# Output projection by token tile, earlier down-projection operands, and the last block's gate moved into its weights

## The chip, the cores and the metric

One core of a Trainium2 chip runs the whole layer. The metric is device time in microseconds (us). The kernel before takes 1323.11 us, the median of three runs (1322.59, 1323.11, 1325.68). Engines are called as in the profile: PE is TensorE (matmuls), PEld its weight loads, DVE VectorE, ACT ScalarE, POOL GpSimd, SP SyncE (here the engine that issues most DMAs).

## The reference, cut to what matters

One transformer layer over 1024 latent tokens of width 1024, in float32. A retention branch and a latent-attention branch come first (not touched by the change); their outputs `y` are concatenated. Then:

```python
x_mid = x + gt_a * (concatenate([y_ret, y_mla]) @ w_out)         # w_out 1024 x 1024
h     = modulate(rms_norm(x_mid, g_ffn), sh_f, sc_f)
x     = x_mid + gt_f * (square(relu(h @ w_ff1)) @ w_ff2)         # 1024 -> 4096 -> 1024
return rms_norm(x, g_final)
```

`gt_a` and `gt_f` are gates: one number per output column (1024 each), the same for all tokens.

## The kernel before, in words

**Products.** Matmul operands are float32 values split into a rounded high part and a low rest. `split` (L102) does that: ACT casts the value (L103), DVE subtracts the cast from it (L104). One product of two operands is then three matmuls (`mm3`, L98 to L100): high by high, high by low, low by high. Tokens are handled in eight tiles of 128 (t = 0 to 7).

**Slots.** Nearly all larger buffers are 4 KB per partition and come from a list of 45 slots (`sl.get`, `sl.put`). A slot is handed out in the order in which slots are given back in the program's text, so a load waits until whoever held its slot before is through. The program is written as one list of steps; the build then lists the instructions of each engine by program order and a modelled time of readiness, so an instruction can stand somewhat ahead of its place in the text. An engine runs its list in order. SP's queue issues loads and stores in its own order, and a load that waits holds up what stands behind it.

**Output projection (630 to about 690 us).** The weights `w_out` are loaded in eight pieces: two column halves hf of 512 columns, four pieces of 256 rows each. `load_wo` loads a piece, POOL multiplies it by the gate `gt_a` of its columns, and `split_wo` (up to three pieces later) splits it. `load_y` loads and splits a token tile of `y`, and loads the tile of `x` into `acc[t]`. `wout_mm(hf, t)` is one group: 24 matmuls of 128x512 for tile t and column half hf, whose result DVE adds into `acc[t]` (the read-out of PSUM, `tt` at L94). The loop goes over both halves, and in each over the tiles: (0, 2) to (0, 7), then (1, 0) to (1, 7); the groups (0, 0) and (0, 1) are done inside the attention before. After a tile's second half come its sum of squares on ACT, the reciprocal root (`rstd_of`: small DVE and ACT operations), the scaling (L1301), the store of `acc[t]` to DRAM as `xm[t]`, and, one tile later, `h2_post`: eight transposes on PE and eight scalings by `Af` (four on DVE at L1064, four on ACT) that write `h` as `h2r`.

**Up products (about 690 to 990 us).** Each 2x2 block product is done by seven products in place of eight (q = 1 to 7, a Strassen scheme). The operands made of `h` are four quarters B11, B12, B21, B22 and four combinations T1 to T4 (`pairop`, L1081, on DVE or POOL, then `bsplit`). B11 and B21 need tokens 0 to 511 only; T1 = B12 - B11, T2 and T4 need tokens 512 to 1023 too. There are 16 blocks p of `w_ff1` with 7 products of 12 matmuls each, in the order `order`; `post1` reads the results out of PSUM, applies the squared relu on ACT and stores the seven left operands of the down products to DRAM (`ud`: a, y, z, w) through SP's queue.

**Down products (about 990 to 1306.6 us).** Four blocks b of `w_ff2` (1024 rows each), seven products each in the order q = 2, 1, 6, 5, 3, 7, 4: 28 steps of 48 matmuls (`mm_2`, four groups k of 12). `load_u` loads the left operand of a step from `ud`, two steps ahead; `load_w2(b)` loads the eight raw weight pieces of a block; `chain_w2` and `chain2_w2` make T1 to T4 of them on POOL (eight operations of 128x1024); `prep2` splits both operands of a step (four casts, four subtractions of 128x1024), one step ahead. After each group DVE adds the result into the quarters of `acc` to which that product belongs (for b = 0 the first is a copy on ACT).

**End.** In the last block the residual tiles `xm` are loaded into `xr_` (`load_xm`) and the gate `gt_f` into `bc[5]` (`load_bc5`). `gated` multiplies a half tile of `acc` by the gate (on DVE or POOL, L1255), adds the residual, and ACT sums the squares; `final` takes the reciprocal root and scales the tile (L1269) into `xr_`, which is stored as the output. Tiles 0 to 3 go through this after product 3, tiles 4 to 7 after products 7 and 4.

## Time and profile before

| | |
|---|---|
| median of three runs | 1323.11 us |
| the profiled execution | 1324.64 us, of which its span is 1322.8 |
| busy share of the span | PE 96%, PEld 82%, DVE 72%, ACT 49%, POOL 19% |
| mean granted clock of PE | 0.989 of full speed |
| last matmul ends | 1306.6 us |

The busy share counts the time in which an engine executes something. An engine that is busy can still be slowed by what it shares with others, so the mean duration of an operation is to be read beside it. A window is a stretch of the span, in us from its start. In a list of waits, "PE ps L99 <- DVE u L104" is PE at line 99, which stood until an operation of DVE at line 104 was done. In a timeline, a row that ends in xN holds N neighbouring instructions, and its second number is their time together.

### The profile page before, as it was taken

How to read it: one execution, taken by the hardware profiler on the slowest of the kernel's cores; microseconds unless marked ns; L12 is line 12 of the kernel's file. 1: busy time of each engine (PE TensorE's matmuls, PEld its weight loads, DVE VectorE, ACT ScalarE, POOL GpSimd, SP SyncE). 2: the span in 40 equal slices, each digit the busy share in tenths (PEclk: the TensorE clock that was granted, in tenths of full speed). 3: DMA queues.
4: the chain of work that ended last, by engine and by line, in shares of the span. 5: the costliest groups of instructions: out<-in, count | busy, mean ns of one | idle time of the engine just before them, and what ended most of it. 6: DMA issues, size and time to landing. Idle time of an engine off the chain costs nothing.

```text
span 1322.8 us, 18063 instructions
## 1 busy us (share of the span) xinstructions
PE 1274.1 (96%) x6665; PEld 1089.7 (82%) x6665; DVE 950.9 (72%) x1828; ACT 654.8 (49%) x1365; POOL 252.9 (19%) x151
## 2 busy tenths in 40 slices
PE   7999999999999999799989999999998999999995
PEld 7788888999989898688777888888886888888884
DVE  5798576665787777985687755565549687888888
ACT  2851257754455555432466655555546543343442
POOL 0100000000000000311343133233315060603501
PEclk9999999999999999999998999999999999999998
DMA  9508401300001003362421544544485635454443
GB/s 346 217 1 279 167 28 53 101 13 1 1 9 37 9 25 102 130 199 96 144 81 64 189 139 157 160 154 134 154 276 182 225 101 175 149 177 143 141 146 128
DMA packets 77547, 166.40 MB, mean 126 GB/s; under 512 B 7689, under 2 KB 27858, under 8 KB 77458
## 3 DMA queue, kind: packets, MB, share of 16 engines
q1 hardware_dynamic: 74338, 156.56, 35.0%
q0 software_dynamic: 2544, 8.15, 1.8%
q8 instruction: 52, 0.85, 0.3%
q10 hardware_dynamic: 576, 0.53, 0.1%
q14 instruction: 37, 0.30, 0.1%
HBM read 123.53 MB, written 41.69 MB: 125 GB/s over the span
## 4 chain that ended last, share of the span: by engine, by line
PE 83%; DVE 11%; DMA 2%; issue 2%; ACT 1%; POOL 0%; POOLq 0%; SPq 0%; DVEq 0%; ACTq 0%
PE ps L99 23%; PE ps L98 23%; PE ps L100 23%; DVE u L104 3%; DVE u L94 3%; PE ps L895 2%; PE ps L280 2%; PE ps L858 1%; PE ps L862 1%; PE ps L860 1%; PE ps L861 1%; PE ps L859 1%; PE ps L238 1%; DVE u L1269 1%; DMA u<-uda 1%
## 5 line engine op out<-in xcount | busy, mean ns | idle before, releaser
L99 PE MATMUL ps<-u,u 128*128 128x512 f32 (+3 forms) x1664 | 615.4, 370 | 10.0 <-DVE u L104 6.8
L98 PE MATMUL ps<-u,u 128*128 128x512 f32 (+3 forms) x1664 | 619.9, 373 | 4.0 <-DVE u L94 2.3
L100 PE MATMUL ps<-u,u 128*128 128x512 f32 (+3 forms) x1664 | 613.9, 369 | 3.6 <-DVE u L104 1.9
L99 PEld LDWEIGHTS ps<-u,u 128*128 128x128 f32 x1664 | 315.1, 189 | 61.8 <-DVE u L104 9.2
L98 PEld LDWEIGHTS ps<-u,u 128*128 128x128 f32 x1664 | 314.8, 189 | 56.7 <-DVE u L94 3.4
L100 PEld LDWEIGHTS ps<-u,u 128*128 128x128 f32 x1664 | 314.7, 189 | 54.6 <-DVE u L104 2.7
L104 DVE TENSOR_TENSOR u<-u,u 128x1024 fp32r<-128x1024 f32 (+4 forms) x213 | 290.7, 1383 | 66.4 <-ACT u L103 55.8
L94 DVE TENSOR_TENSOR u<-ps,u 128x512 f32<-128x512 f32 (+4 forms) x334 | 210.8, 650 | 122.7 <-ACT u L1153 56.8
L103 ACT CAST u<-u 128x1024 fp32r<-128x1024 f32 (+3 forms) x215 | 197.2, 941 | 190.5 <-PE ps L99 46.4
L1081 POOL TENSOR_TENSOR u<-u,u 128x1024 f32<-128x1024 f32 x34 | 100.9, 2990 | 182.9 <-ACT u L103 98.9
L863 DVE TENSOR_REDUCE mx<-ps 128x1 f32<-128x512 f32 (+1 forms) x96 | 55.4, 595 | 26.7 <-PE ps L862 26.5
L94 DVE TENSOR_TENSOR u<-u,u 128x512 f32<-128x512 f32 x72 | 50.6, 702 | 33.0 <-ACT u L1131 18.4
L897 ACT CAST u<-ps 128x512 fp32r<-128x512 f32 (+1 forms) x96 | 45.3, 530 | 22.9 <-PE ps L895 22.8
L103 ACT CAST u<-tmp 128x512 fp32r<-128x512 f32 x64 | 37.8, 621 | 37.3 <-DVE u L104 31.9
L1095 POOL TENSOR_TENSOR tmp<-u,u 128x512 f32<-128x512 f32 x16 | 20.7, 1296 | 176.2 <-DMA u<-in_w_ff_dram 172.8
L933 POOL DMA_DIRECT2D y_dram<-tmp x7 | 5.4, 765 | 253.5 <-ACT tmp L931 253.5
L874 ACT ACTIVATE u<-ps,nm 128x512 f32<-128x512 f32 x64 | 43.7, 693 | 17.8 <-DVE nm L867 17.8
L104 DVE TENSOR_TENSOR u<-tmp,u 128x512 fp32r<-128x512 f32 x64 | 43.8, 722 | 11.8 <-ACT u L103 9.0
L1130 ACT ACTIVATE u<-u 128x512 f32<-128x512 f32 x64 | 40.1, 628 | 19.0 <-DVE u L94 18.8
L1131 ACT ACTIVATE u<-u 128x512 f32<-128x512 f32 x64 | 40.3, 631 | 1.4
L858 PE MATMUL ps<-u,u 128*128 128x512 f32 (+1 forms) x96 | 37.5, 391 | 2.7 <-ACT u L874 2.5
L427 DVE SCALAR_TENSOR_TENSOR u<-u,sc,u 128x1024 f32<-128x1024 f32 x28 | 35.9, 1281 | 4.2 <-DMA u<-in_w_ada_dram 3.7
(210 smaller groups left out, 1339.4 us busy)
## 6 DMA issues: line engine op xcount, KB each, us to landing
u<-in_w_ff_dram SPq DMA_DIRECT2D x64, 512.0 KB, 4.4
u<-in_w_ada_dram SPq DMA_DIRECT2D x48, 512.0 KB, 5.3
u<-in_x_dram SPq DMA_DIRECT2D x16, 512.0 KB, 5.6
udy<-u SPq DMA_DIRECT2D x16, 512.0 KB, 3.0
udz<-u SPq DMA_DIRECT2D x16, 512.0 KB, 3.4
udw<-u SPq DMA_DIRECT2D x16, 512.0 KB, 3.9
u<-udy SPq DMA_DIRECT2D x16, 512.0 KB, 6.5
u<-udz SPq DMA_DIRECT2D x16, 512.0 KB, 4.6
```

The costliest lines, as they stand in the source:

```text
L94: V.tensor_tensor(out=o, in0=a, in1=b, op=op)
L98: T.matmul(ps, lhsT=lh, rhs=rh, start=start, stop=False, **kw)
L99: T.matmul(ps, lhsT=lh, rhs=rl, start=False, stop=False, **kw)
L100: T.matmul(ps, lhsT=ll, rhs=rh, start=False, stop=stop, **kw)
L103: S.copy(out=hi, in_=raw)
L104: (eng or V).tensor_tensor(out=lo, in0=raw, in1=f(hi), op=ALU.subtract)
L858: T.matmul(ps[:, 0:n], lhsT=qh, rhs=kh, start=True, stop=False)
L863: V.reduce_max(out=mx[:, kb:kb + 1], in_=ps[:, 0:n], axis=AX.X)
L874: S.activation(out=dst[kb], in_=ps[:, 0:n], func=AF.Exp, scale=SCALE, bias=nm, accum_out=su[:, kb:kb + 1])
L897: S.copy(out=hi, in_=ps[:, 0:m, :])
L1081: eng.tensor_tensor(out=o[v][0], in0=a[v][0], in1=b[v][0], op=op)
L1131: S.activation(out=ap, in_=ap, func=AF.Square)
```

## The change

Three edits, in one diff.

1. *Output projection.* The groups keep their contents and get another order, `wseq`: (0, 2), (0, 3), then (1, 0) to (1, 3), then the two halves of tile 4, of tile 5, of tile 6 and of tile 7 next to each other. The four loads of the second column half's weights are issued before the first two of these groups, and the loads of `y`, the first splits of `h` (`bsplit`), the first loads of `w_ff1` and their preparation move to places in the new sequence.
2. *Down operands.* The left operand of the first down step and the first weight quarter are loaded 11 products ahead of the end of the up products instead of 6, the rest 6 and 4 ahead of it. The first step's splits are placed 6 products ahead of that end instead of 3, and the second step's, which stood at the first down step, 2 ahead of it.
3. *Gate.* For the last block, `gate_w2` multiplies the eight raw weight pieces by the gate `gt_f` on POOL, so that the block's products need no gate. What the first three blocks have summed up in `acc` is multiplied by the gate and added to the residual by `to_mid` on DVE: halves of tiles 0 to 3 at the last two steps of the third block, of tiles 4 to 7 at the first two steps of the last. The gate's load, and the loads of the last block's weights in each block (at product 5 in place of product 3), move accordingly. `gated` is gone; `squares` and `final` are left for the end, and the output is scaled in place in `acc`.

```diff
--- before.py
+++ after.py
@@ -1172,8 +1172,8 @@
 
     w2r, w2v = {}, w_ff2.rearrange("(g i p) c -> i p g c", i=2, p=P)
 
-    def load_w2(b):
-        for q in ("B21", "B11", "B12", "B22"):
+    def load_w2(b, qs=("B21", "B11", "B12", "B22")):
+        for q in qs:
             i, j = BH[q]
             w2r[b, q] = [sl.get((2, 512)) for _ in range(GB // 2)]
             for v, r in enumerate(w2r[b, q]):
@@ -1250,15 +1250,6 @@
 
     fs = {}
 
-    def gated(t, cs, eng=None):
-        w, xw = acc[t][0][:, cs], xr_[t][0][:, cs]
-        (eng or V).tensor_tensor(out=w, in0=w, in1=bc[5][0][:, cs], op=ALU.mult)
-        tt(w, w, xw, ALU.add)
-        if t not in fs:
-            fs[t] = sm(2, "ss2")
-        h = cs.start // 512
-        S.activation(out=xw, in_=w, func=AF.Square, accum_out=fs[t][:, h:h + 1])
-
     def final(t):
         ss = fs[t]
         tt(ss[:, 0:1], ss[:, 0:1], ss[:, 1:2], ALU.add)
@@ -1266,59 +1257,59 @@
         n = 2 if t == NT - 1 else 1
         for q in range(n):
             cs = slice(q * 1024 // n, (q + 1) * 1024 // n)
-            V.scalar_tensor_tensor(out=xr_[t][0][:, cs], in0=acc[t][0][:, cs], scalar=r, in1=gfin[0][:, cs],
+            V.scalar_tensor_tensor(out=acc[t][0][:, cs], in0=acc[t][0][:, cs], scalar=r, in1=gfin[0][:, cs],
                                    op0=ALU.mult, op1=ALU.mult)
-            (nc.sync, nc.scalar)[q].dma_start(out=out[0, t * P:(t + 1) * P, cs], in_=xr_[t][0][:, cs])
+            (nc.sync, nc.scalar)[q].dma_start(out=out[0, t * P:(t + 1) * P, cs], in_=acc[t][0][:, cs])
 
     lag = Lag(1)
-    for hf in range(2):
-        for t in range(NT):
-            if hf == 0:
-                for _ in range(2):
-                    mod_step()
-                    mod_load(4, 32)
-                if 4 <= t + 2 < NT:
-                    load_y(t + 2)
-                if t in (3, 4, 5, 6):
-                    load_wo(1, t - 3)
-                if t == 7:
-                    wlag.flush()
-            if hf or t >= 2:
-                wout_mm(hf, t, pG)
-            if hf == 1:
-                sl.put(*yt_[t])
-                if t == 0:
-                    Af = const.tile([P, KD], F32, name="Af")
-                    V.scalar_tensor_tensor(out=Af, in0=mcol[4], scalar=1.0, in1=col("gf"), op0=ALU.add, op1=ALU.mult)
-                if t % 4 == 0:
-                    for u in range(4):
-                        h2r[u, t // 4] = sl.get((2, 512))
-                sq = sl.get((1024,))
-                ss = sm(1, "ss")
-                S.activation(out=sq[0], in_=acc[t][0], func=AF.Square, accum_out=ss)
-                nc.gpsimd.dma_start(out=xm[t], in_=acc[t][0])
-                r = rstd_of(ss, D, 1, "x")
-                V.tensor_scalar(out=sq[0], in0=acc[t][0], scalar1=r, scalar2=None, op0=ALU.mult)
-                sl.put(acc[t])
-                wt = slice((t % 4) * P, (t % 4 + 1) * P)
-                lag.push(lambda t=t, sq=sq, wt=wt: h2_post(t, sq, wt))
-                if t == 2:
-                    mod_fin(fins.popleft())
-                if t == 4:
-                    load_w1(0)
-                    load_w1(1)
-                if t == 5:
-                    bsplit("B21", braw("B21"))
-                    bsplit("B11", braw("B11"))
-                if t == 6:
-                    chain_w1(0)
-                    for q in (2, 1):
-                        for p in range(2):
-                            prep1(p, q) if (p, q) != (1, 1) else None
-        for u in range(4):
-            sl.put(*wo.pop((hf, u)))
-        if hf == 0:
+    wseq = [(0, 2), (0, 3), (1, 0), (1, 1), (1, 2), (1, 3)] + [(hf, t) for t in range(4, NT) for hf in range(2)]
+    for n, (hf, t) in enumerate(wseq):
+        if n < 8:
+            for _ in range(2):
+                mod_step()
+                mod_load(4, 32)
+        if n < 2:
+            load_wo(1, 2 * n)
+            load_wo(1, 2 * n + 1)
+            wlag.flush()
+        if n < 2 or (hf, t) in ((0, 4), (0, 5)):
+            load_y({0: 4, 1: 5}.get(n, t + 2))
+        if n == 2:
             sl.put(bc[2])
+        wout_mm(hf, t, pG)
+        if n == 9:
+            while fins:
+                mod_fin(fins.popleft())
+        if hf == 1:
+            sl.put(*yt_[t])
+            if t == 0:
+                Af = const.tile([P, KD], F32, name="Af")
+                V.scalar_tensor_tensor(out=Af, in0=mcol[4], scalar=1.0, in1=col("gf"), op0=ALU.add, op1=ALU.mult)
+            if t % 4 == 0:
+                for u in range(4):
+                    h2r[u, t // 4] = sl.get((2, 512))
+            sq = sl.get((1024,))
+            ss = sm(1, "ss")
+            S.activation(out=sq[0], in_=acc[t][0], func=AF.Square, accum_out=ss)
+            nc.gpsimd.dma_start(out=xm[t], in_=acc[t][0])
+            r = rstd_of(ss, D, 1, "x")
+            V.tensor_scalar(out=sq[0], in0=acc[t][0], scalar1=r, scalar2=None, op0=ALU.mult)
+            sl.put(acc[t])
+            wt = slice((t % 4) * P, (t % 4 + 1) * P)
+            lag.push(lambda t=t, sq=sq, wt=wt: h2_post(t, sq, wt))
+        if (hf, t) == (0, 5):
+            bsplit("B21", braw("B21"))
+        if (hf, t) == (1, 5):
+            load_w1(0)
+        if (hf, t) == (0, 6):
+            bsplit("B11", braw("B11"))
+        if (hf, t) == (1, 6):
+            load_w1(1)
+            chain_w1(0)
+            for p, q in ((0, 2), (1, 2), (0, 1)):
+                prep1(p, q)
+    for k_ in list(wo):
+        sl.put(*wo.pop(k_))
     lag.flush()
 
     pF = Ring(list(range(8)))
@@ -1363,48 +1354,78 @@
             bsplit("T3", b12, True)
         if s == 3:
             bsplit("B22", b22, True)
+        if s == len(order) - 11:
+            load_w2(0, ("B21",))
+            load_u(*steps2[0])
         if s == len(order) - 6:
-            load_w2(0)
-            load_u(*steps2[0])
+            prep2(*steps2[0])
+            load_w2(0, ("B11",))
             load_u(*steps2[1])
+        if s == len(order) - 4:
+            load_w2(0, ("B12", "B22"))
         if s == len(order) - 3:
-            prep2(*steps2[0])
             chain_w2(0)
+        if s == len(order) - 2:
+            prep2(*steps2[1])
 
     pF = Ring(list(range(8)))
     acc = {}
     for t in range(NT):
         acc[t] = sl.get((1024,))
+    HALF = slice(0, 512), slice(512, 1024)
+
+    def gate_w2(b):
+        for q in ("B21", "B11", "B12", "B22"):
+            g = bc[5][0][:, HALF[BH[q][1]]].unsqueeze(1).broadcast_to([P, 2, 512])
+            for r in w2r[b, q]:
+                G.tensor_tensor(out=r[0], in0=r[0], in1=g, op=ALU.mult)
+
+    def to_mid(t, h, eng):
+        if t not in xr_:
+            load_xm(t)
+        w = acc[t][0][:, HALF[h]]
+        eng.tensor_tensor(out=w, in0=w, in1=bc[5][0][:, HALF[h]], op=ALU.mult)
+        tt(w, w, xr_[t][0][:, HALF[h]], ALU.add)
+        if h == (t < 4):
+            sl.put(xr_.pop(t))
+
+    def squares(t, h):
+        if t not in fs:
+            fs[t] = small.tile([P, 2], F32, name=f"fs{t}", tag=f"fs{t}", bufs=1)
+        S.activation(out=tmp(), in_=acc[t][0][:, HALF[h]], func=AF.Square, accum_out=fs[t][:, h:h + 1])
+
     for s, (b, q) in enumerate(steps2):
+        last = b == NB - 1
         if s + 2 < len(steps2):
             load_u(*steps2[s + 2])
         if s + 1 < len(steps2):
-            if q == 4 and b + 1 < NB:
-                pass
-            prep2(*steps2[s + 1])
+            if s > 0:
+                prep2(*steps2[s + 1])
             if steps2[s + 1][1] == 2:
                 chain_w2(b + 1)
-        if q == 3 and b + 1 < NB:
+        if b == NB - 2 and q == 2:
+            load_bc5()
+        if q == 5 and b + 1 < NB:
             load_w2(b + 1)
-        last = b == NB - 1
-        if last and q == 1:
-            load_bc5()
+        if b == NB - 2 and q == 7:
+            gate_w2(b + 1)
         if last and q == 6:
             gfin = sl.get((1024,))
             nc.sync.dma_start(out=gfin[0], in_=A["g_final"].partition_broadcast(P))
-        if last and q == 5:
-            for t in range(NT):
-                load_xm(t)
         for k in range(4):
             mm_2(b, q, k)
+            if b == NB - 2 and q in (7, 4):
+                to_mid(k, q == 4, V)
+            if last and q in (2, 1):
+                to_mid(4 + k, q == 2, V)
             if last and q == 3:
-                gated(k, slice(0, 512), G)
-                gated(k, slice(512, 1024), V)
+                squares(k, 0)
+                squares(k, 1)
                 final(k)
             if last and q == 7:
-                gated(4 + k, slice(512, 1024), G)
+                squares(4 + k, 1)
             if last and q == 4:
-                gated(4 + k, slice(0, 512))
+                squares(4 + k, 0)
                 final(4 + k)
         for x_ in ab.pop((b, q)):
             for h_ in x_:
```

## Rows read from the trace of the kernel before

**Rows 1.** The busy table: engine, busy us (share of the span), instructions.

```profile
PE 1274.1 (96%) x6665; PEld 1089.7 (82%) x6665; DVE 950.9 (72%) x1828; ACT 654.8 (49%) x1365; POOL 252.9 (19%) x151
```

**Rows 2.** Stretches: start:end, length, busy PE PEld DVE ACT POOL, clock, DMA share, GB/s.

```profile
1186.90:1197.80 10.90, 10.90 (x50) 9.02 (x49) 8.31 (x10) 4.44 (x6) 0.00 (x0) 1.00 0.21 55
1176.00:1252.20 76.20, 76.20 (x338) 63.08 (x337) 62.47 (x61) 26.79 (x27) 27.28 (x10) 1.00 0.45 146
690.00:715.00 25.00, 19.14 (x66) 14.22 (x66) 24.35 (x25) 16.34 (x24) 7.01 (x3) 0.86 0.18 56
985.00:1015.00 30.00, 25.23 (x101) 19.42 (x100) 24.77 (x16) 15.39 (x21) 23.92 (x8) 0.94 0.52 180
1015.00:1306.60 291.60, 291.52 (x1286) 240.76 (x1284) 236.25 (x261) 119.94 (x147) 82.51 (x32) 1.00 0.48 161
1306.60:1322.80 16.20, 0.00 (x0) 0.00 (x0) 12.35 (x38) 4.18 (x16) 0.00 (x0) 0.66 0.33 130
```

**Rows 3.** Waits of PE, 690 to 715: us in total, times, longest.

```profile
PE ps L99 <- DVE u L104: 4.2, 2, 2.8
```

**Rows 4.** Waits of PE, 985 to 1015.

```profile
PE ps L99 <- DVE u L104: 2.6, 2, 2.4
PE ps L100 <- DVE u L104: 1.9, 1, 1.9
```

**Rows 5.** DVE in order of time, 676 to 697: start, us, operation, instructions.

```profile
677.29 0.68 DVE L94 TENSOR_TENSOR u<-ps,u 128x512 f32<-128x512 f32 x1
...
684.44 1.36 DVE L1064 TENSOR_SCALAR u<-ps,Af,mcol 128x128 f32<-128x128 f32 x4
...
688.16 3.35 DVE L104 TENSOR_TENSOR u<-u,u 128x1024 fp32r<-128x1024 f32 x1
...
694.77 1.21 DVE L104 TENSOR_TENSOR u<-u,u 128x1024 fp32r<-128x1024 f32 x1
```

**Rows 6.** ACT in order of time, 984 to 1000; in brackets idle before, releaser.

```profile
995.28 1.04 ACT L103 CAST u<-u 128x1024 fp32r<-128x1024 f32 x1 [1.74 <-DMA u<-udy]
```

**Rows 7.** Groups, 1176 to 1252.2: busy us, mean ns, idle before, releasers.

```profile
L104 DVE TENSOR_TENSOR u<-u,u 128x1024 fp32r<-128x1024 f32 x29 | 43.5, 1518 | 7.2 <-ACT u L103 6.4 <-PE ps L99 0.4
...
L94 DVE TENSOR_TENSOR u<-ps,u 128x512 f32<-128x512 f32 x31 | 20.6, 683 | 7.5 <-PE ps L100 7.4
```

**Rows 8.** Line 1081 in the whole span: ns shortest/median/longest, first and last start.

```profile
L1081 POOL TENSOR_TENSOR u<-u,u x34: 2362/3260/3454, 687.2 to 1231.8; 128x1024 f32<-128x1024 f32 x34
```

**Rows 9.** SP's queue in order of time, 985 to 987 and 1170 to 1200.

```profile
985.93 0.96 SPq L1205 DMA_DIRECT2D u<-udy  x1
...
1176.75 21.66 SPq L1181 DMA_DIRECT2D u<-in_w_ff_dram  x8
```

**Rows 10.** PE in order of time, 991 to 993.

```profile
991.68 0.50 PE L98 MATMUL ps<-u,u 128*128 128x512 f32 x1 [0.23 <-ACT u L103]
```

**Rows 11.** DVE in order of time, 1310 to the end.

```profile
1317.64 1.41 DVE L1269 SCALAR_TENSOR_TENSOR u<-u,xr,u 128x512 f32<-128x512 f32 x2
```

**Rows 12.** ACT in order of time, 1311 to 1314.

```profile
1312.61 0.63 ACT L1260 ACTIVATE u<-u 128x512 f32<-128x512 f32 x1 [0.50 <-DVE u L94]
```

**Rows 13.** DVE in order of time, 629 to 634.

```profile
631.41 0.15 DVE L108 TENSOR_SCALAR xv<-ss 128x1 f32<-128x1 f32 x1 [1.22 <-ACT u L1298]
...
632.84 0.75 DVE L1301 TENSOR_SCALAR u<-u,xr 128x1024 f32<-128x1024 f32 x1
```

**Rows 14.** POOL in order of time, 985 to 1012 and 1200 to 1220.

```profile
986.17 24.00 POOL L1081 TENSOR_TENSOR u<-u,u 128x1024 f32<-128x1024 f32 x8 [27.01 <-PE ps L100]
...
1208.41 6.79 POOL L1081 TENSOR_TENSOR u<-u,u 128x1024 f32<-128x1024 f32 x2 [49.43 <-ACT u L103]
```

**Rows 15.** DVE in order of time, 984 to 1013.

```profile
991.66 6.22 DVE L104 TENSOR_TENSOR u<-u,u 128x1024 fp32r<-128x1024 f32 x2 [5.23 <-ACT u L103]
...
1008.43 3.96 DVE L104 TENSOR_TENSOR u<-u,u 128x1024 fp32r<-128x1024 f32 x2
```

## The prediction

> **What bounds the kernel now.** The busy table comes first. TensorE (PE) is busy 96% of the span, VectorE (DVE) 72% [rows 1]: only time in which PE stands still, or runs slowly, can be won, and DVE is the engine that can take PE's place. The stretches of the span show where PE stands still [rows 2]. From 1015.0 to 1306.6 it never does: 1286 matmuls in 291.6 us, 0.2267 each, so a down step (48 matmuls) takes 10.9 and an up product (12) 2.72. Three places are left. Between output projection and up products (690 to 715) PE is idle 25.0 - 19.14 = 5.9 us; its granted clock of 0.86 there means 7.0 us at the lower of its two levels, 1.2 in place of 2.4 GHz, which costs 3.5. Between up and down products (985 to 1015) it is idle 4.8, and 0.94 of the clock costs 1.8. Behind the last matmul, at 1306.6, come 16.2 us without PE. Together 32 of 1322.8 us: the upper limit of this change, but for some short waits before 690.
>
> The waits say on what. In the first gap PE waits for a subtraction of DVE, 4.2 of 5.9 us [rows 3]; in the second too, 2.6 + 1.9 [rows 4].
>
> **Part 1, output projection by token tile.** What PE waits for at 691 and 696 is T1, made of the second token half, so of tile 7 too. Its way on DVE after the last projection group: read-out 677.29, h2 written at 685.8, difference, split of the first half done at 691.5, of the second at 695.98 [rows 5]: 18.7 after the read-out. The change takes work off this way (tile 6's transposes and its four scalings, 1.36 as at 684.44, come a group earlier) but no link of it, and what covers it is the same four products and half a fifth, 12.2 us, with tile 7's transposes. I book -2: the 1.36 and some of the slow clock. Bounds: -9.4 if T1 comes in time; +5.7 if the second column half's weights, now wanted after two groups instead of after six, come late (one POOL product of up to 3.45, a cast 1.04, a subtraction 1.21 [rows 6 to 8]). I don't expect the latter: their slots are the 3rd to 16th taken in this stage, where before the first of the four was the 17th.
>
> **Part 2, down operands during the last up products.** Before, the last raw operand of the first step leaves SP's queue at 985.93, behind stores of the up stage; its cast waits for it until 995.28 [rows 6, 9], and PE's first down matmul starts at 991.68 [rows 10] only to stand. The change asks for it five products (13.6 us) earlier, so it lands about 982, and its four subtractions lie beside the last up products. Counted through the list of 45 slots, the second step's operand gets a slot only when the stores of up block 14 are through (near 988), so lands at 993 to 997 and is split by 1001 to 1003; PE wants it at 991.3 + 10.9 = 1002.2. POOL's difference chain, eight operations, starts later for the same reason, and its T2 is wanted at 1013. I book -5 of the 6.6 (bounds 0 and -6.6). SP carries the same loads and stores in another order; nothing else waits on it there.
>
> **Part 3, the gate in block 3's weights.** The tail first. Before, after the last matmul DVE runs read-out, gate product, addition and the last scaling of four tiles; the last scaling ends at 1319.05 and the run 3.7 behind it [rows 11]. After, tile 7 needs: read-out 0.68 [rows 7], square 0.63 [rows 12], the chain to the reciprocal root (1.43 where nothing disturbs it, 631.41 to 632.84 [rows 13]) with one small addition more, 0.2, two halves of the scaling 1.41, 0.7 for hand-overs and the square's sum, then 3.7: 8.7 us. Tile 6's scaling (1.3) may stand in front. So -7.5 or -6.2; I book -7.
>
> Now the price. Block 3's weights get eight products of 128x1024 on POOL. The 16 gate products (eight of them on POOL before) and 16 additions on the outputs, all of 128x512, are now all DVE's, and their place goes from the last three steps to the last two of block 2 and the first two of block 3. POOL has room (27 of 76 us [rows 2]). The trouble is DVE. Undisturbed, a subtraction of 128x1024 takes 1.21, but over this stretch the mean is 1.52 [rows 7], and while POOL works without a break from 986 to 1010 [rows 14], two of them take 6.22 [rows 15]: each waits for a POOL operation, whose own length goes from 2.36 to 3.45 [rows 8]. A read-out of PSUM (0.68) is not slowed.
>
> The Trainium skill has a rule on this (SBUF — State Buffer, section "SBUF: two separate sides"): VectorE and GpSimd share one port pair under an exclusive lock, and against a VectorE operation with two SBUF inputs the loser blocks for the whole instruction. The trace agrees in kind, 6.22 for two; taken at its word the rule leads to rival (b).
>
> Count from the fourth step of block 2 (1186.9) to where block 3's second step needs its last operands (1241.3 + 1.4): 55.8 us. Why from there: by the list of slots, six of block 3's eight raw weight loads now wait for slots that the third step frees, at 1186.9 (before, they left one by one from 1176.75 to 1198.4 [rows 9]), so six gate products fall behind it, and the difference chain's eight operations wait for slots freed near 1218. DVE has 16 subtractions (1.13 from start to start), 20 read-outs (0.60) and 16 gate products and additions (0.60): 18.1 + 12.0 + 9.6 = 39.7. To that the locks of 14 POOL operations. Low end: as in this stretch before, where 62.5 us of DVE time hold 29 x 1.13 + 31 x 0.60 = 51.4 of work [rows 2, 7], so 11 for ten POOL operations, 1.1 each: 15.4, in all 55.1, no stall. High end: 2.36 each: 33.0, in all 72.7, a stall of 17. Nearest row: from 991.66 to 1012.4 DVE was as full as it will be here and did seven subtractions and three read-outs, 9.7 of work, in 20.7 [rows 15]: 11 for 6.6 POOL operations, 1.65 each. That gives 23.1, in all 62.8, 7 too many. Nor can the operands be readied ahead to soften it: before, they were split 5 to 17 us early, but the slots of the second step's now come from the residual tiles, free only when the additions are through. Behind a blocked DVE operation stands the subtraction that PE needs, and PE stops at block 3's first or second step. I book +7.
>
> Sum: -2 - 5 - 7 + 7 = -7 on the profiled execution, 1324.64 (span 1322.8; it is 1.5 above the median of the three runs shown). On the median: 1323.11 - 7 = **1316.1**; own range 1311 to 1319.
>
> **Rivals.** (a) DVE's lead hides part 3's price (its low end): -14, 1309. For it: POOL stands idle for 49 us ahead of 1208 [rows 14], where gate products can run as the loads land, and DVE has 2.6 us over in a step such as that at 1186.9 [rows 2]. Against: the late slots. (b) On the other side, slower: the lock at full length. 17 us of stall between 1230 and 1260; then two more steps hold 8 subtractions, 8 read-outs and 16 gate products and additions, 23.4 in 21.8, another 1.6; and such a stop lets the clock fall once, half of the first gap's 3.5. +20.3 in place of +7: 1323.1 - 14 + 20.3 = 1329. It decides from 14 us of stall, 2.15 per POOL operation. For it: two subtractions in 6.22; against: read-outs and waits for loads lie under POOL's time for nothing. (c) Part 2 doesn't do what it says: the second step's operand and T2 come late by what the first step gained. With the stall of 7: 1323.1 - 2 - 7 + 7 = 1321.
>
> **How the numbers follow.** About 0.3%, 4 us, can be told from no change. The forecast has 0.45, (a) 0.20, (b) 0.19, (c) 0.16. The first two are faster, (b) is slower, (c) nearly all within 4 us: faster 0.65, same 0.15, slower 0.20. The range goes from (a) with some of part 1's bound, 1305, to just short of (b), 1328.
>
> **What would show it.** In the changed kernel's stretches and waits: idle PE between up and down under 2 us (part 2); 8 to 10 us from the last matmul to the end (tail); a mean subtraction of DVE over 2 us from block 2's fourth step to block 3's second, and a PE wait for it of some us at block 3's first two steps (price); the wait for T1 still there (part 1). No PE wait among the down steps means (a), over 14 us of them (b). The prediction is wrong altogether if PE waits for weights at the third projection group.

## The result, and the profile after

The changed kernel is slower: 1336.72 us (median of four runs, 1334.56 to 1340.73) against 1322.85 for the kernel before beside it, a ratio of 1.0106 with a 95% interval of 1.0076 to 1.0136. I had forecast 1316.1, with a range of 1305 to 1328. Its profiled execution took 1337.57, its span 1335.8.

The busy table of the changed kernel; it answers to [rows 1]:

```profile
PE 1275.3 (95%) x6665; PEld 1090.4 (82%) x6665; DVE 958.1 (72%) x1836; ACT 654.3 (49%) x1365; POOL 255.7 (19%) x151
```

The amount of work is nearly the same (DVE 7 us more); PE stands still longer. Both programs have the same 6665 matmuls, so the same matmul, counted from the end, can be looked up in both traces. How much later it starts after the change:

| at (us in the trace before) | later by | part |
|---|---|---|
| 288 to 551 | 1.1 | nothing is changed yet |
| 732, first up products through | 5.0 | part 1: +3.9 |
| 1023, second down step through | -2.4 | the gap between up and down is gone: -7.4 |
| 1034, third down step through | 8.4 | a new stop: +10.8; part 2: +3.4 |
| 1216, ahead of the third block's last step | 8.4 | |
| 1306, last matmul | 20.0 | another stop: +11.6 |
| end of the span | 12.9 | the tail: -7.1; part 3: +4.5 |

These are differences of two single traces. In the thirteen runs below that leave the projection as it was, the stretch from 551 to 732 comes out between 3.3 us shorter and 1.0 longer than in this one trace of the kernel before, so the +3.9 is uncertain by some 2 us. Between 732 and 1034 the runs that leave that stretch as it was agree within 1 us, and from there to the last matmul within 0.2.

The stretches of the changed kernel, which answer to [rows 2] (start:end, length, busy PE PEld DVE ACT POOL, clock, DMA share, GB/s):

```profile
690.00:720.00 30.00, 21.81 (x86) 16.73 (x84) 26.65 (x26) 18.63 (x26) 12.08 (x4) 0.89 0.16 52
985.00:1015.00 30.00, 30.00 (x134) 24.68 (x133) 18.59 (x17) 15.71 (x23) 14.50 (x6) 1.00 0.77 263
1015.00:1045.00 30.00, 20.97 (x85) 16.95 (x84) 23.57 (x19) 14.51 (x17) 6.76 (x3) 0.83 0.54 180
1225.00:1255.00 30.00, 21.41 (x85) 16.55 (x84) 30.00 (x25) 6.10 (x6) 20.97 (x8) 0.89 0.12 40
1326.60:1335.80 9.20, 0.00 (x0) 0.00 (x0) 4.92 (x17) 1.53 (x6) 0.00 (x0) 0.73 0.44 171
```

985 to 1015, where PE had been idle 4.8 us, is full. The next 30 us hold the new stop, 1225 to 1255 the second. The tail is 9.2 us and not 16.2.

Waits of PE in the changed kernel: 575 to 640 (two rows), 690 to 720 (two), 985 to 1300 (the last):

```profile
PE ps L98 <- DVE u L94: 4.9, 2, 3.2
PE ps L238 <- DVE u L1296: 3.8, 2, 3.3
...
PE ps L98 <- ACT u L103: 4.2, 2, 3.6
PE ps L99 <- DVE u L104: 4.0, 2, 2.6
...
PE ps L98 <- DVE u L94: 17.8, 5, 9.0
```

All 17.8 us of the down products are waits for line 94, the read-out of PSUM, and none for a subtraction. The products 1, 6 and 7 of a group share a bank, and product 4 gets the same bank after product 7, in a ring of eight. So the first matmul of product 6 waits until DVE has read product 1, and the first of product 4 until DVE has read product 7.

**The stop at the third down step.** POOL, 985 to 1025, against [rows 14]; then ACT, 1002 to 1009; then DVE, 1000 to 1031:

```profile
1000.42 21.34 POOL L1081 TENSOR_TENSOR u<-u,u 128x1024 f32<-128x1024 f32 x8 [34.87 <-DMA u<-in_w_ff_dram]
```

```profile
1006.84 1.05 ACT L103 CAST u<-u 128x1024 fp32r<-128x1024 f32 x1 [3.71 <-DMA u<-udz]
```

```profile
1007.92 3.17 DVE L104 TENSOR_TENSOR u<-u,u 128x1024 fp32r<-128x1024 f32 x1 [5.67 <-ACT u L103]
1011.01 2.90 DVE L94 TENSOR_TENSOR u<-u,u 128x512 f32<-128x512 f32 x1
1013.84 2.88 DVE L94 TENSOR_TENSOR u<-u 128x512 f32<-128x512 f32 x1
1016.65 5.67 DVE L94 TENSOR_TENSOR u<-u,u 128x512 f32<-128x512 f32 x2
...
1029.22 1.28 DVE L94 TENSOR_TENSOR u<-ps,u 128x512 f32<-128x512 f32 x2
```

POOL's differences start at 1000.4 and not at 986.2, since B12 and B22 land late. DVE first waits 5.7 us for a late cast of the third step (its operand lands late too), and then makes the four combinations of the last up block beside the differences: 0.68 us each where nothing disturbs them (around 983 in the trace before), 2.9 here. The read-out that PE wants stands behind, at 1029.2.

**The stop in the last step of the third block.** POOL and then DVE, 1225 to 1250:

```profile
1226.67 16.30 POOL L1081 TENSOR_TENSOR u<-u,u 128x1024 f32<-128x1024 f32 x6 [12.12 <-issue]
```

```profile
1226.88 2.75 DVE L94 TENSOR_TENSOR u<-u,u 128x512 f32<-128x512 f32 x1
1229.55 1.27 DVE L94 TENSOR_TENSOR u<-ps,u 128x512 f32<-128x512 f32 x2
1230.74 4.46 DVE L94 TENSOR_TENSOR u<-u,u 128x512 f32<-128x512 f32 x2
1235.13 1.27 DVE L94 TENSOR_TENSOR u<-ps,u 128x512 f32<-128x512 f32 x2
1236.33 4.44 DVE L94 TENSOR_TENSOR u<-u,u 128x512 f32<-128x512 f32 x2
1240.69 3.36 DVE L104 TENSOR_TENSOR u<-u,u 128x1024 fp32r<-128x1024 f32 x1
```

The five additions and the subtraction take 15.0 us and not 5 x 0.68 + 1.21 = 4.6. The read-outs between them, with one operand in PSUM, keep their time (1.27 for two). Two of POOL's operations by themselves, and PE's first matmuls of product 4 in the last two groups:

```profile
1229.15 2.72 POOL L1081 TENSOR_TENSOR u<-u,u 128x1024 f32<-128x1024 f32 x1
1231.83 2.83 POOL L1081 TENSOR_TENSOR u<-u,u 128x1024 f32<-128x1024 f32 x1
```

```profile
1236.46 0.50 PE L98 MATMUL ps<-u,u 128*128 128x512 f32 x1 [2.53 <-DVE u L94]
1245.31 0.79 PE L98 MATMUL ps<-u,u 128*128 128x512 f32 x1 [5.79 <-DVE u L94]
```

The two additions that start at 1230.74 take 1.67 and 2.87 us. They end at 1232.42 and 1235.21, each 0.55 behind the end of one of these POOL operations (1231.87 and 1234.66); the other three additions end 0.55 behind one too, the subtraction 1.09. What an operation loses is thus what is left of the POOL operation that it meets. PE loses 11.6, slow clock included.

**The projection.** DVE, 575 to 584 and 608 to 620, and PE, 614 to 620:

```profile
580.28 2.29 DVE L104 TENSOR_TENSOR u<-u,u 128x1024 fp32r<-128x1024 f32 x1 [2.70 <-ACT u L103]
...
612.25 2.61 DVE L427 SCALAR_TENSOR_TENSOR u<-u,sc,u 128x1024 f32<-128x1024 f32 x2 [1.53 <-DMA u<-in_w_ada_dram]
614.78 0.68 DVE L94 TENSOR_TENSOR u<-ps,u 128x512 f32<-128x512 f32 x1
```

```profile
618.96 1.09 PE L238 MATMUL ps<-ident,u 128*128 128x128 f32 x8 [3.25 <-DVE u L1296]
```

Tile 0's second half is through on PE about 610.3 (5.4 us, one group, ahead of the stop), but its read-out waits behind sums of the last modulation vector (line 427) until 614.8; its transposes come one group later and stop PE for 3.3.

**From the projection to the up products.** PE's waits of over 1 us before (690 to 715), then all of them after (690 to 720):

```profile
691.56 0.50 PE L99 MATMUL ps<-u,u 128*128 128x512 f32 x1 [1.40 <-DVE u L104]
696.03 0.50 PE L99 MATMUL ps<-u,u 128*128 128x512 f32 x1 [2.81 <-DVE u L104]
707.64 1.22 PE L98 MATMUL ps<-u,u 128*128 128x512 f32 x2 [1.29 <-ACT u L103]
```

```profile
697.35 0.50 PE L99 MATMUL ps<-u,u 128*128 128x512 f32 x1 [1.39 <-DVE u L104]
702.17 0.50 PE L98 MATMUL ps<-u,u 128*128 128x512 f32 x1 [0.63 <-ACT u L103]
705.30 0.50 PE L99 MATMUL ps<-u,u 128*128 128x512 f32 x1 [2.62 <-DVE u L104]
709.35 1.22 PE L98 MATMUL ps<-u,u 128*128 128x512 f32 x2 [3.55 <-ACT u L103]
```

PE waits for T1 in the first two rows before (4.2 us) and in the first row after (1.4): T1 does come earlier. Counted by the matmuls, the two rows behind it are waits for T2, and the last is for a cast of a left operand that stands behind DVE's splits. By the same matmul the change is 4.6 us late at 677, 0.1 ahead at 700 and 5.0 late at 715: what T1 gains, DVE's next operands take back.

### The profile page after: what moved, and what is told of

It is laid out like the page before. It is cut to its first block, busy times and chain, and to the rows that moved or that the text cites. A ratio compares the mean times of both kernels' runs of the same rounds, so it can differ in the third digit from the quotient of the medians.

```text
span 1335.8 us, 18065 instructions
## 1 busy us (share of the span) xinstructions
PE 1275.3 (95%) x6665; PEld 1090.4 (82%) x6665; DVE 958.1 (72%) x1836; ACT 654.3 (49%) x1365; POOL 255.7 (19%) x151
## 5 line engine op out<-in xcount | busy, mean ns | idle before, releaser
L104 DVE TENSOR_TENSOR u<-u,u 128x1024 fp32r<-128x1024 f32 (+4 forms) x213 | 285.1, 1357 | 74.2 <-ACT u L103 65.8
L1081 POOL TENSOR_TENSOR u<-u,u 128x1024 f32<-128x1024 f32 x34 | 96.4, 2859 | 148.8 <-PE ps L99 97.7
L94 DVE TENSOR_TENSOR u<-u,u 128x512 f32<-128x512 f32 x72 | 65.7, 917 | 28.0 <-ACT u L1131 19.1
```

Of the source, the lines that this page charges most:

```text
L94: V.tensor_tensor(out=o, in0=a, in1=b, op=op)
L104: (eng or V).tensor_tensor(out=lo, in0=raw, in1=f(hi), op=ALU.subtract)
L1081: eng.tensor_tensor(out=o[v][0], in0=a[v][0], in1=b[v][0], op=op)
```

## The experiments

The kernel before stood beside each run on the same chip; ratios are to it.

| run | median us | ratio (95%) |
|---|---|---|
| e1 projection only | 1327.57 | 1.0048 (1.0032 to 1.0064) |
| e2 down operands only | 1327.07 | 1.0039 (1.0023 to 1.0054) |
| e3 gate only | 1327.04 | 1.0043 (1.0027 to 1.0058) |
| e4 all quarters early | 1322.29 | 1.0003 (0.9992 to 1.0014) |
| e5 gate, no differences | 1315.02 | 0.9949 (0.9933 to 0.9965) |
| e6 gate, no gate products | 1324.26 | 1.0011 (0.9998 to 1.0024) |
| e7 projection, late sums | 1325.33 | 1.0029 (1.0016 to 1.0042) |
| e8 weights before splits | 1334.38 | 1.0092 (1.0075 to 1.0109) |
| e9 left operand first | 1322.62 | 0.9999 (0.9987 to 1.0010) |
| e10 T3 difference on DVE | 1325.21 | 1.0017 (1.0006 to 1.0028) |
| e11 gate in T4 only | 1324.23 | 1.0008 (0.9998 to 1.0018) |
| e12 down, no differences | 1315.24 | 0.9946 (0.9928 to 0.9963) |
| e13 projection, no up differences | 1317.39 | 0.9957 (0.9942 to 0.9971) |
| e14 gate, additions apart | 1328.08 | 1.0043 (1.0028 to 1.0058) |
| e15 projection, no second gate | 1322.93 | 1.0006 (0.9994 to 1.0019) |
| e16 down, differences on DVE | 1315.64 | 0.9941 (0.9919 to 0.9963) |
| e17 gate, differences on DVE | 1317.43 | 0.9958 (0.9946 to 0.9971) |
| e18 both on DVE | 1310.03 | 0.9897 (0.9880 to 0.9914) |

### Each part alone

```diff
+    wseq = [(0, 2), (0, 3), (1, 0), (1, 1), (1, 2), (1, 3)] + [(hf, t) for t in range(4, NT) for hf in range(2)]
```

> The kernel before with the new order of the output projection and nothing else. Theory (each part loses by itself, at its own place, as the trace of the changed kernel shows it): about +4 us, 1327; PE stops for 2 to 3 us ahead of tile 0's transposes near 615, for 2 to 4 us behind read-outs near 580 and 595, and the waits for T1 between 690 and 715 stay as long as before (about 9 us in all). Rival (the parts collide through the list of slots, each alone does what the prediction booked): -2, 1321, the transposes without a wait over 1 us.

```diff
+        if s == len(order) - 11:
+            load_w2(0, ("B21",))
+            load_u(*steps2[0])
...
+        if s == len(order) - 2:
+            prep2(*steps2[1])
```

> The kernel before with the down operands loaded and split earlier and nothing else. Theory (each part loses by itself): the 6.6 us between up and down products go, and a stop of 9 us and 2 us of slow clock come at the third down step, because the third and fourth weight quarters land about 12 us later than before, POOL's eight differences run that much later, and four additions of 128x512 on DVE take 2.8 us each beside them: +3 to +4, 1326. Rival (collision through the slots): the prediction's -5 or at least the bound 0, 1318 to 1323, with no stop over 3 us in the first four down steps.

```diff
+        if b == NB - 2 and q == 7:
+            gate_w2(b + 1)
...
+            if last and q in (2, 1):
+                to_mid(4 + k, q == 2, V)
```

> The kernel before with the gate put into the last block's weights and nothing else. Theory (each part loses by itself): the tail behind the last matmul is 9 us instead of 16.2, and PE stops for 9 to 12 us between the last step of the third block and the second step of the last, behind read-outs that wait behind additions of 2.8 us each: +4 to +5, 1327.5. Rival (collision through the slots): the prediction's 0, 1323, with a stop of at most 7 us.

Each is slower by itself, by 0.39 to 0.48%; the sum, 1.30%, is near the change's 1.06%. The stops stand at their places: 3.4 and 3.3 us in the projection, one of 8.2 at the third down step, three of 7.1 in all in the last step of the third block. The parts do not have to meet to lose.

### Part 2: order of the loads, or POOL beside DVE

The cuts of e4, e12 and e16 are against e2.

```diff
             prep2(*steps2[0])
-            load_w2(0, ("B11",))
+            load_w2(0, ("B11", "B12", "B22"))
             load_u(*steps2[1])
-        if s == len(order) - 4:
-            load_w2(0, ("B12", "B22"))
```

> Only the earlier down operands, but the third and fourth weight quarters (B12, B22) are loaded with the second, 6 products ahead of the end and not 4. Theory (the late quarters hold up POOL's eight differences, and with them the third step's left operand, whose slot a difference still reads, and DVE's additions beside them): POOL's first difference starts at about 987 and not at 1000, the stop of 8.3 us at the third down step falls below 2, and the run gains about 10 us on the part alone: 1316 to 1318. Rival (the splits of the second step, now ahead on DVE, and the additions of the last up block stand in front of the read-out whatever POOL does): the stop stays over 5 us, 1323 to 1327.

Between the two: a stop of 4.8 us is left and the run is level with the kernel before. The first difference came at 986.75, but the others waited for the loads, as POOL shows (980 to 1015):

```profile
986.75 2.40 POOL L1081 TENSOR_TENSOR u<-u,u 128x1024 f32<-128x1024 f32 x1 [26.08 <-DMA u<-in_w_ff_dram]
993.35 18.88 POOL L1081 TENSOR_TENSOR u<-u,u 128x1024 f32<-128x1024 f32 x7 [4.19 <-DMA u<-in_w_ff_dram]
```

Two more orders: e8 is e4 with two lines exchanged, e9 the kernel before with two lines exchanged:

```diff
-            prep2(*steps2[0])
-            load_w2(0, ("B11",))
+            load_w2(0, ("B11", "B12", "B22"))
+            prep2(*steps2[0])
```

> Only the earlier down operands; the second to fourth weight quarters are loaded 6 products ahead of the end and, unlike the run before it, ahead of the first step's splits, so that the splits' eight slots are not handed out first. Theory (the order in which slots are handed out makes the weights late, and by that POOL's differences): the differences run from 987 without the break of 4 us that the second one had, the stop at the third step (5.0) falls below 2, 1316 to 1319. Rival (the last up block's additions and the splits still stand beside the differences, whenever these start): the stop stays at 3 us or more, 1320 to 1323.

```diff
+            load_u(*steps2[0])
             load_w2(0)
-            load_u(*steps2[0])
```

> The kernel before with one pair of lines exchanged: 6 products ahead of the end the first step's left operand is loaded ahead of the eight weight pieces and not behind them. Theory (SP's order alone made the first stop of 2.9 us): the cast that waited until 995 runs before 990, the first stop goes, the second of 2.1 stays or shrinks: 2 to 5 us gained, 1317 to 1320. Rival (the weights now land later and hand the wait on, as in the changed kernel): no gain, 1322 or more, with a stop of over 3 us at one of the first three steps.

Both theories fell. PE's waits from 980 to 1300, e8 (three rows) and e9 (two):

```profile
PE ps L98 <- DVE u L94: 5.7, 1, 5.7
PE ps L99 <- DVE u L104: 4.9, 1, 4.9
PE ps L98 <- ACT u L1149: 2.6, 1, 2.6
```

```profile
PE ps L99 <- DVE u L104: 5.3, 3, 1.9
PE ps L100 <- DVE u L104: 1.3, 1, 1.3
```

None of the orders tried brings the stretch clearly below the 6.6 us of the kernel before (e4 loses 6.1, e9 6.9); they only choose the step that pays.

```diff
+        if b > 0:
             pairop(G, r("T1"), r("B12"), r("B11"), ALU.subtract)
...
+        else:
+            for v in range(n):
+                S.copy(out=r("T1")[v][0], in_=r("B12")[v][0])
+                S.copy(out=r("T2")[v][0], in_=r("B22")[v][0])
```

> Only the earlier down operands, with POOL's eight differences of the first down block left out (T1 and T2 are copies of B12 and B22 made on ACT, T3 and T4 are B12 and B21 as they are, so that block's products are not the layer's). Theory (DVE is full from 985 to 1030, and beside each difference one of its operations takes 2.8 to 3.4 us: no order of loads helps, only fewer differences beside it): the stop of 8.3 us at the third step falls below 1.5, 1315 to 1317. Rival (left operands and weights land late whatever POOL does): a stop of 4 us or more stays, 1320 to 1325.

The stop is gone (0.3 us is left), and the run is 0.54% faster than the kernel before. But this run takes away the work, the waiting beside POOL and the late slots at once. e16 keeps the work:

```diff
+        eng = V if b == 0 else G
-        pairop(G, r("T1"), r("B12"), r("B11"), ALU.subtract)
+        pairop(eng, r("T1"), r("B12"), r("B11"), ALU.subtract)
...
```

> Only the earlier down operands, with the eight differences of the first down block on DVE in place of POOL. Nothing is left out. Theory (side by side: a difference beside DVE costs it about 2 us, on DVE it costs 1.1, and with the differences gone DVE was busy about two thirds of 985 to 1045): the stop at the third step falls from 8.3 to below 2, 1316 to 1319. Rival (the work itself: 9 us more on DVE stand in front of the same read-outs): a stop of 4 us or more, 1321 or more.

As the theory had it. The stretch 985 to 1040 of e2, e12 and e16, and three operations of e16's DVE:

```profile
985.00:1040.00 55.00, 46.84 (x196) 38.10 (x196) 40.10 (x33) 27.84 (x37) 21.62 (x8) 0.91 0.71 240
```

```profile
985.00:1040.00 55.00, 54.67 (x241) 44.85 (x240) 34.40 (x36) 38.13 (x50) 0.00 (x0) 1.00 0.71 246
```

```profile
985.00:1040.00 55.00, 54.82 (x242) 44.95 (x241) 42.74 (x44) 35.16 (x46) 0.00 (x0) 1.00 0.73 251
```

```profile
996.90 5.76 DVE L1081 TENSOR_TENSOR u<-u,u 128x1024 f32<-128x1024 f32 x5
...
1006.31 0.69 DVE L94 TENSOR_TENSOR u<-u,u 128x512 f32<-128x512 f32 x1 [0.78 <-ACT u L1131]
```

Five differences take DVE 1.15 us each, and the combination behind them has its 0.69 again. In e16 DVE is busier than in e2 (42.7 against 40.1 us; the same time, in which PE gets 46 more matmuls done) and PE does not wait. One thing besides the engine differs: the first load of the third step's left operand leaves SP's queue at 995.9 in e16 and at 998.6 in e2. So some of what e16 gains may be that operand and not the undisturbed DVE; the two were not taken apart. That also corrects my expectation of e12: DVE was not full here (34.4 of 55 without the differences); its list was late.

### Part 3: which POOL operations, and where

The cuts of e5, e6, e14 and e17 are against e3. e5 leaves out the last block's differences as e12 does the first's (`b < NB - 1`); e6 cuts the gate products:

```diff
-                G.tensor_tensor(out=r[0], in0=r[0], in1=g, op=ALU.mult)
+                G.tensor_tensor(out=r[0][:, :, 0:8], in0=r[0][:, :, 0:8], in1=g[:, :, 0:8], op=ALU.mult)
```

> Only the gate in the weights, with POOL's eight differences of the last block left out: T1 and T2 are copies of B12 and B22 made on ACT, T3 and T4 are B12 and B21 as they are, so the last block's products are not the layer's. Theory (each addition of 128x512 on DVE waits for a whole difference of POOL): the additions go from 2.8 to 0.7 us, the stops of 2.7 and 4.4 us around the start of the last block fall below 1 in all, 1316 to 1318. Rival (DVE simply has too many operations there, or the residual tiles and operands come late): stops of 4 us or more stay, 1321 or more.

> Only the gate in the weights, with POOL's eight gate products of the last block cut to 8 of 512 columns, so most of the last block's weights carry no gate. Theory (these products run where DVE has time over; the differences make the stop): the stops around the start of the last block stay at 5 us or more in all, at most 3 less than with them, 1324 to 1327. Rival (they put DVE behind, as my count for the prediction had it: 8 of 14 POOL operations): the stops fall by 6 or more, 1316 to 1320.

e5 has no wait of PE at all between 1150 and 1300, e6 still 5.4 us. The rows of additions between 1214 and 1240 (busy us, mean ns), e3 and e5:

```profile
L94 DVE TENSOR_TENSOR u<-u,u 128x512 f32<-128x512 f32 x7 | 14.8, 2146 | 0.0
```

```profile
L94 DVE TENSOR_TENSOR u<-u,u 128x512 f32<-128x512 f32 x12 | 8.1, 696 | 0.0
```

So without the differences there is no stop, and the gate products are worth 2.8 us of the time (e3 less e6). They also set its place: without them DVE is ahead, the read-outs of the third block's last step come in time, and 4.8 of e6's 5.4 us are a wait for a subtraction at the second step of the last block (1244.4), where the prediction had looked for it.

```diff
-            if b == NB - 2 and q in (7, 4):
-                to_mid(k, q == 4, V)
-            if last and q in (2, 1):
-                to_mid(4 + k, q == 2, V)
+            if b == NB - 2 and q in (6, 7):
+                to_mid(k, q == 7, V)
+            if last and q in (6, 5):
+                to_mid(4 + k, q == 6, V)
```

> Only the gate in the weights, with the gate products and additions on the sums moved away from POOL's differences: tiles 0 to 3 at the third and sixth step of the third block in place of the sixth and seventh, tiles 4 to 7 at the third and fourth step of the last block in place of the first and second. Nothing is left out. Theory (the stops are these operations waiting beside the differences, with DVE full): the stops of 7.6 us and 2 us of slow clock fall below 3 in all, the tail stays at 9, 1316 to 1320. Rival (the residual tiles now hold four slots two steps longer, the last block's weights and left operands come late): a stop of 4 us or more stays, 1321 to 1327.

The rival held: two waits of 10.4 us in all. The residual tiles' loads left SP's queue at 1174.2 (in e3 at 1204.8) and the last block's first weights at 1178.2 (in e3 at 1164.0). So all eight gate products came together from 1187.7, the last six as below; POOL worked with one break of 6.8 us until 1235, and from 1211 to 1237 DVE was busy 25.97 of 26.0 us (POOL, 1170 to 1260):

```profile
1192.89 18.14 POOL L1375 TENSOR_TENSOR u<-u,u 128x1024 f32<-128x1024 f32 x6 [0.43 <-DMA u<-in_w_ff_dram]
1217.78 17.12 POOL L1081 TENSOR_TENSOR u<-u,u 128x1024 f32<-128x1024 f32 x6 [6.75 <-issue]
```

The tail alone, with two gate products, against the kernel before:

```diff
         w2r[b, "T4"] = w2r.pop((b, "B21"))
+        if b == NB - 1:
+            for r in w2r[b, "T4"]:
+                G.tensor_tensor(out=r[0], in0=r[0], in1=bc[5][0][:, 0:512].unsqueeze(1).broadcast_to([P, 2, 512]), op=ALU.mult)
```

> The kernel before with the gate in one right operand of the last block alone: T4, whose product is the last to be added, gets two gate products on POOL; the sums of tiles 4 to 7 without it are gated and added to the residual a step earlier, those of the first columns of tiles 0 to 3 two steps earlier. Theory (the tail is worth 7 us, and what the change paid for it was eight gate products, the additions' place beside the differences and the slots): the tail falls from 16.2 to about 9.5, no stop over 1 us comes ahead of it, 1315 to 1318. Rival (DVE is full in the last four steps, and the work only queues there): the tail stays over 12, 1319 to 1323.

The rival again: the tail is 13.2 us, and PE waits 2.9 ahead of it, for read-outs behind the products and additions that were moved there. DVE's work at the end is worth moving only to where DVE has time.

```diff
+        eng = V if b == NB - 1 else G
...
-            if last and q in (2, 1):
-                to_mid(4 + k, q == 2, V)
+            if last and q in (6, 5):
+                to_mid(4 + k, q == 6, V)
```

> Only the gate in the weights, with the eight differences of the last block on DVE in place of POOL, and the additions on tiles 4 to 7 at the third and fourth step of the last block in place of the first and second. Nothing is left out. Theory (side by side; DVE has in the critical steps as much as in the run without differences, 9.0 more by them and 9.6 less by the additions): the stops of 7.6 us fall below 2, the tail grows to 9 to 12, 1316 to 1320. Rival (DVE was full there already without the differences, so their 9 us show on PE): stops or a longer tail of 5 us or more in all, 1321 or more.

PE's waits from 1150 to 1310 are 0.3 us. Two things differ from e3 here, the engine of the differences and the place of the gating and adding of tiles 4 to 7; their shares were not taken apart.

### Part 1: what stands ahead of the read-outs, and T1

The cuts of e7 and e13 are against e1, that of e15 against e7.

```diff
-        if n < 8:
+        if 5 <= n < 10:
             for _ in range(2):
                 mod_step()
```

> Only the new order of the projection, with the last modulation vector's sums (line 427, DVE, 1.28 us each and waiting for weight loads) moved from the first five groups to groups 6 to 10. Theory (these sums stand in DVE's list ahead of the first second-half read-outs, so tile 0 is ready late): the read-out of tile 0 comes 2 to 4 us earlier, the stop of 3.4 us ahead of its transposes falls below 1, 1324 to 1325. Rival (the splits of the second half's weights, waiting for POOL's gate products, stand there): the stop stays over 2.5 us, 1327.

```diff
+        m = 8 if hf else 512
-        G.tensor_tensor(out=r[0], in0=r[0], in1=bc[2][0][:, hf * 512:(hf + 1) * 512].unsqueeze(1).broadcast_to([P, 2, 512]),
+        G.tensor_tensor(out=r[0][:, :, 0:m], in0=r[0][:, :, 0:m], in1=bc[2][0][:, hf * 512:hf * 512 + m].unsqueeze(1).broadcast_to([P, 2, m]),
```

> The new order of the projection with the late modulation sums, and the gate products of the second column half of the projection's weights cut to 8 of 512 columns (so most of that half carries no gate). Theory (the stop of 3.0 us near 580 is a read-out that stands behind a subtraction that waits for, and then beside, such a product): the stop falls below 1, 1322 to 1324. Rival (other work ahead of the read-out on DVE): it stays over 2, 1325.

e7: tile 0's stop fell from 3.4 to 0.5, but tile 1's transposes now wait 1.8; 2.2 us gained, which the intervals of e1 and e7 do not quite tell apart. e15: the wait of 2.9 near 580 fell to 1.0, another 2.4 us. e1 and e15 are clearly apart (1.0048 and 1.0006). With both taken away, part 1 is level with the kernel before and not ahead of it: the waits behind 690 are those of e1, 7.9 to 8.2 us in all against 5.7 in the kernel before.

```diff
-    pairop(V, b11, b12, b11, ALU.subtract)
-    bsplit("T1", b11)
+    bsplit("T1", b12)
+    bsplit("T2", b22)
-    pairop(G, b12, b22, b12, ALU.subtract)
...
```

> Only the new order of the projection, with all differences of the up products' right operands left out (T1 and T2 are B12 and B22, T3 and T4 are B12 and B21 as they are, so five of seven up products are not the layer's); the splits still need tile 7. Theory (DVE is full from 685 to 715: the six differences of 1.2 us each and POOL's two beside them are more than four and a half products cover): the waits between 690 and 715, 9.1 us with 2 us of slow clock, fall by 6 to 10 us, 1318 to 1321. Rival (the way from tile 7's last group is too long by its number of steps, whatever DVE has besides): the first wait of 1.5 stays and the sum falls by less than 4, 1324 to 1327.

All waits there are gone: between 677 and 732 of the trace before, PE gains 10.7 us, where e1 had lost 1.4. Tile 7's way keeps its read-out, transposes and splits, but loses T1's difference, so this run shortens the way a little as well as taking work off DVE. Moving only POOL's share to DVE, on the kernel before, does not help:

```diff
-    pairop(G, b12, b22, b12, ALU.subtract)
...
+    pairop(V, b12, b22, b12, ALU.subtract)
```

> The kernel before with the T3 difference of the up products (two operations of 128x1024) made by DVE behind its own differences and not by POOL beside them. Theory (the waits for T1 that neither kernel gets rid of come from DVE operations of 1.2 us that take 2.8 to 3.4 beside this POOL work): the two waits of 1.6 and 3.0 us fall by 2 to 4 in all, 1318 to 1320. Rival (the way from the last projection group to T1 is long by its number of steps): they stay within 1 us, and DVE's 2.4 us more come on top, 1322 to 1324.

The rival: the waits are 7.8 us, the first one shorter, the later ones longer. In this stretch DVE has next to no break, 24.35 of 25.0 us busy [rows 2]. That DVE pays for the differences on either engine fits both runs; it is argued and not shown by itself.

### The version that comes out

> The kernel before with the earlier down operands and the gate in the weights, the differences of the first and the last down block on DVE, the additions on tiles 4 to 7 two steps later, and the old order of the projection. Nothing is left out. Theory (the parts act at separate places): the gains of 7 and 5 us add up, 1309 to 1312, no stop over 1.5 us behind 985, a tail of 9 us. Rival (the list of slots shifts between the two and makes operands late): a new stop of 3 us or more, 1313 to 1317.

Its edits are those of e16 and e17 together. It takes 1310.03 us, 1.0% less than the kernel before (0.9880 to 0.9914) and 2% less than the change. Its stretches between up and down, between the last two blocks, and behind the last matmul:

```profile
985.00:1015.00 30.00, 30.00 (x133) 24.50 (x132) 27.36 (x29) 19.85 (x29) 0.00 (x0) 1.00 0.81 268
1200.00:1245.00 45.00, 44.56 (x195) 36.28 (x195) 44.97 (x56) 15.80 (x17) 0.00 (x0) 1.00 0.42 151
1297.60:1307.50 9.90, 0.00 (x0) 0.00 (x0) 5.62 (x17) 1.53 (x6) 0.00 (x0) 0.73 0.41 159
```

POOL does nothing in these stretches. In the second DVE is busy 44.97 of 45.00 us, and PE 44.56: a DVE without a break does not by itself make PE wait.

## Why the prediction was wrong

**Part 1, forecast -2, measured +3.9 (e1's six runs: 0.48%, 6 us): the step failed.** It followed T1's way, and there it was right: from tile 7's read-out (681.5) to T1's last split (697.3) it now takes 15.8 us and not 18.7, and PE's wait for T1 falls from 4.2 to 1.4. But it took that wait for the end of the matter. The operands behind T1 in DVE's list then come late, and PE's waits in this stretch grow from 5.7 to 8.2 us. And it asked of the rest only whether PE waits for weights. The second-half groups, whose results PE needs one group later, now come after two groups and not after six, while the side work on DVE stayed beside the first groups: sums for the modulation, and splits that wait for POOL. e7 and e15 take back 2.2 and 2.4 us of it. The bound of +5.7 had named that POOL product, cast and subtraction and put them aside; PE did not wait for the weights themselves, but for a read-out that stood behind the subtraction. The 3.5 us of slow clock that the prediction counted in this gap are no fixed sum: from 685 to 720 the granted clock is 0.90 in its trace, and 0.85 to 1.00 in the thirteen runs with the same code in that stretch.

**Part 2, forecast -5 with bounds of 0 and -6.6, measured +3.4: the step failed, and its bounds excluded a loss without a reason.** The 6.6 went: the gain there is 7.4, where 5 were booked. The text even said that POOL's differences start later, and charged nothing for what DVE would then have beside them. The term that was missing is the 10.8 us at the third step; e12 and e16 show that it goes when the differences are not on POOL. Rival (c) had the right doubt, that the wait is handed on, and too small a size.

**Part 3, the tail: right.** -7 was booked, -7.1 measured; the last scaling, [rows 11] before, now starts at 1330.95 and the run ends 3.4 behind its end.

**Part 3, the price: right mechanism, wrong size, +7 booked and +11.6 measured.** The price of a POOL operation was not the mistake: 10.4 us of DVE time for six of them, 1.7 each, against the 1.65 I took. That the two agree is partly luck: in the row from which I took it, DVE met 5.8 POOL operations and not 6.6 (POOL's last one ends at 1010.17 [rows 14]), so the row gives 1.9, and my count with 1.9 gives 10.5 and not 7. The mistake was to spread 14 of them over 56 us with the room that DVE has on the way. The gate products were mostly covered (e6); the six differences fell into 16 us in which the list of DVE has no room, and there nearly all of their price shows on PE. The place was off too, by a step and by the operation: I expected the stop at the first or second step of the last block and at a subtraction, whose lead of 5 to 17 us I had read. It came in the last step of the third block, at the read-out, which has no lead at all and stands behind a blocked DVE operation.

The Trainium skill (SBUF — State Buffer, section "SBUF: two separate sides") says that the loser of the shared port pair blocks for the whole instruction. The trace agrees: all five additions end 0.55 us behind the end of a POOL operation, whether they take 1.65 us or 2.87; the short ones merely met it later, since two read-outs ran first. That is also why the mean price, 1.7 us, is below a whole POOL operation of 2.4 to 2.8. The Trainium skill (SBUF — State Buffer, section "Summary: rules for kernel authors") says to schedule whichever of the two is off the critical path. Here the read-outs behind the DVE operations were on it, and in e16, and with moved additions in e17, it was better to have no second engine there.

**The chances.** I gave 0.20 to slower, nearly all of it rival (b)'s 0.19, and that for part 3 alone, at 1329. All three parts lost, each by itself in e1 to e3, and I gave a chance to one of them only.

## What to carry to other kernels

Where a DVE operation with two SBUF operands would run beside POOL, count for DVE's operation what is left of the POOL operation that it meets (1.7 us on average at the second stop here), and compare with doing POOL's work on DVE (1.15 us for 128x1024): where DVE's list stood between PE and its next bank, the second engine cost more than it took over. Price such a stop over the shortest stretch in which PE needs DVE, not over the average, and look for the operation that has no lead, the read-out. And when a load or a group is moved earlier, ask what it now runs beside, what it is now behind, and which operand PE will wait for next, not only when it arrives.

## What the runs showed that I had not expected

- An addition of 128x512 beside POOL takes 1.65 to 1.67 and 2.87 us in turn, always to 0.55 behind the end of a POOL operation, and POOL's own operation goes from 2.4 to 2.8; beside subtractions of 128x1024 it goes to 3.4.
- Read-outs from PSUM keep 0.64 to 0.68 in the midst of this, and ACT's casts their 1.05.
- A stop can be undone in one place and come back in another with nearly the same size: between the up products and the fourth down step, four orders of the same loads (before, e2, e4, e9) lose 6 to 10 us, and one (e8) over 17.
